# All tiles of z in pairs, scans beside 16 gate tiles at a falling pace, one feed-forward split sooner

## The chip, the cores and the metric

The kernel runs on one core of one Trainium2 chip. The metric is the device time of one execution in microseconds. TensorE does all matmuls and transposes; VectorE (DVE in the rows), ScalarE (ACT) and GpSimd (POOL) work beside it on tiles in SBUF and on PSUM banks; each of these engines works through its own instructions in the order in which the program issues them. SyncE (SP), ScalarE and GpSimd also issue DMAs. The kernel fixes the order on each engine by hand: instructions stand on an engine in the order in which the Python program calls them.

## The reference, cut to what matters

```
h  = rmsnorm(x, norm_mix_w)                       # x: 1024 rows x 1024
u  = h @ w_in                                     # z 2048, xbc 3072, dt 32, s_b, s_c, s_x, g_a, g_b 1024 each
xbc = silu(causal_conv(xbc))                      # 4 taps -> xs (2048), B, C (4 groups x 128)
y  = ssd_chunked_scan(xs, dt, a, B, C) + d_skip * xs
y  = y * silu(z)                                  # per group of 512 columns:
y  = y * rsqrt(mean(y*y) + eps) * ssd_norm_w
branch_a = y @ w_ssd_proj
branch_b = (s_b * causal_conv(s_c * s_x)) @ w_sconv_proj
h1 = x + (sigmoid(g_a) * branch_a + sigmoid(g_b) * branch_b) @ w_o
out = rmsnorm(h1 + swiglu(rmsnorm(h1)), final_norm_w)   # swiglu: silu(h@w_gate)*(h@w_up) @ w_down, 2816 wide
```

Everything is float32.

## The kernel before

**Numbers.** Every float32 product is computed as three matmuls of float32r (hi·hi, hi·lo, lo·hi: `mm3`, L80 to L83, and `mmc`, L678 to L681). Each operand is split for it by `split`: ScalarE copies the high part (L73, L76), VectorE subtracts it from the source (L74, L77). SBUF is dealt out in 47 pages of 128x1024 float32 from one pool, PSUM in 8 banks of 128x512.

**Stages**, with the time of the profiled execution.

- *Start* (0 to about 20 us): `x` is loaded by rows (the first four tiles by L231 on SP), `rows_sq` and `rows_scale` form the norm on ScalarE and VectorE, and the rows are transposed.
- *Pairs* (to 619 us): two tiles of 128 columns of `w_in` are taken together and multiplied with the normed, transposed `x` by the Strassen-Winograd scheme, in 7 products of 4 k x 3 matmuls instead of 2 tiles x 48. A `Pair` loads its two slabs, forms the sums of the blocks, splits them and evicts each product. `slots` lists all products: those of the first three z pairs interleaved, then the pairs of `rest_p` one by one, which takes in turn one of `conv_p` (xbc) and one of `free_p` (s_c, s_x, s_b, and the other z pairs, which are its end). There are 30 pairs, 6 of them for z (12 of its 16 tiles); the last three in order are z pairs.
- *Direct* (619 to 952.6 us): the last four tiles of z and the 16 tiles of g_a and g_b are computed by `direct_tile`, each in two halves of 512 rows, each half 8 k x 3 matmuls. A z tile is evicted raw by `z_raw` and every two tiles ScalarE applies silu to both; a gate tile is evicted raw and goes to DRAM. The high part of the next tile is split in the first half at k = 1, the low part at k = 7.
- *Scans* (`scans`) run beside the direct tiles. An item is one group (g of 4) and one block of 128 rows (c of 8). `part1` (L408 on) transposes xs, multiplies B with C, prepares the operands `bh`, `bl` (B^T) and `xw` (weighted xs); ahead of the next item, `prep2` (L396 to L400) computes decays on ScalarE. `part2` (L459 on) reads the former state (`poff`), forms the new one (`pst`, evicted to `st` by L482 in the first item of a group) and adds the parts of y. After every fourth item `norm` (L502 on) multiplies with silu(z), sums squares (`pq`), takes the reciprocal root (`rstd_of`, L99 to L107), transposes it (`prt`, L532), sends it to DRAM and back as a broadcast (`rbc`, two DMAs of POOL), scales y with it (L543), and at the end of a group forms four sums t1 and t2 and stores them. These generators wait in a list and advance by one step at each scan step.
- *Merge* (952.6 to 1250 us): the products with w_sconv_proj, w_ssd_proj and w_o (`gv`, `gy`, `go` in one `Stream`, Strassen-Winograd by blocks of 512), in chunks of 24 matmuls. After each chunk what is left of the scans and norms is pumped. The list `chunks` says what is split ahead. During `go`, the last, `early_weights` (L1327 to L1344) loads and splits the first weights of the feed-forward.
- *Feed-forward* (to the end): `ffn_phase`; `steps[s]` holds, for product s, the split of its weights, its matmuls and its eviction. 

**What sets the pace of the scans.** `direct_tile` counts turns (one turn is one k: three matmuls) and gives out the next scan step (`pump_scan`) whenever the count asks for it:

```
turn, SCAN_STEPS = [0, 0], 2 * G * NT + 1
due = turn[0] * SCAN_STEPS // (len(direct) * 2 * KT - 4)
if due > turn[1]:
    turn[1] = due
    pump_scan()
```

So 65 steps are spread evenly over 316 of the 320 turns. Steps 1 and 2 are the first halves of items 0 and 1, and from there second and first halves take turns (step 3 the second half of item 0, step 4 the first half of item 2).

## Time and profile before

| | |
|---|---|
| time, median of 3 runs | 1910.57 us (1910.33 to 1910.74) |
| the profiled execution's own time | 1910.68 us |
| its span in the profile | 1908.9 us |
| TensorE busy (PE) | 1879.7 us, 98% |
| weight loads of TensorE (PEld) | 81% |
| VectorE busy | 1299.4 us, 68% |
| ScalarE busy | 970.6 us, 51% |
| GpSimd busy | 9% |

The span runs from the first to the last recorded instruction. "Busy" is an average over the stages; the rows of a stage further down say more. A line number such as L679 is the line of the kernel whose instruction it is, and names such as `gb_8196` are tiles with a running number. TensorE takes up its matmuls overlapped, so that the length of one row is more than the distance to the next.

### The profile page before, as it was taken

What the parts mean: (1) busy time and instruction counts of PE and PEld (TensorE: products, weight loads), DVE (VectorE), ACT (ScalarE), POOL (GpSimd) and SP (SyncE); (2) the same over time, 40 slices, a digit from 0 to 9 for tenths busy, and PEclk for the clock granted to TensorE, in tenths of its full rate; (3) what the DMA queues carried; (4) which work ended last, traced back from release to release, by engine and by line L of the source; (5) the groups of instructions that cost most, each with busy time, mean ns of one, the idle gap of its engine ahead of it and who ended that gap; (6) DMA issues with size and microseconds to landing.
All of it is one profiled execution on the core that took longest, in us unless ns stands there. A gap on an engine that the chain in (4) does not pass through costs nothing.

```text
span 1908.9 us, 24143 instructions
## 1 busy us (share of the span) xinstructions
PE 1879.7 (98%) x8905; PEld 1545.3 (81%) x8905; DVE 1299.4 (68%) x1688; ACT 970.6 (51%) x1541; POOL 169.7 (9%) x196
## 2 busy tenths in 40 slices
PE   7999999999999999999999999999999999999998
PEld 5688888888888888888878888887888888888886
DVE  7667878777785678889878548877444444456465
ACT  5545454444444987877665454464333333345333
POOL 1010111101100000101010000101211121100000
PEclk9999999999999999999999999999999999999999
DMA  5197999978959656778798665917988888867552
GB/s 181 48 275 173 240 230 236 240 187 226 264 149 288 223 194 219 251 250 269 261 321 311 226 208 203 229 80 171 215 193 220 195 193 192 232 257 286 190 196 110
DMA packets 341190, 411.97 MB, mean 216 GB/s; under 512 B 17384, under 2 KB 223936, under 8 KB 341072
## 3 DMA queue, kind: packets, MB, share of 16 engines
q1 hardware_dynamic: 284400, 308.59, 50.0%
q0 software_dynamic: 48608, 72.47, 20.9%
q10 hardware_dynamic: 8064, 29.36, 3.8%
q8 instruction: 70, 1.15, 0.2%
q14 instruction: 48, 0.39, 0.1%
HBM read 320.56 MB, written 143.15 MB: 243 GB/s over the span
## 4 chain that ended last, share of the span: by engine, by line
PE 92%; DVE 4%; ACT 2%; DMA 1%; issue 1%; SPq 0%; ACTq 0%; DVEq 0%
PE pb L679 5%; PE pb L680 5%; PE pb L681 5%; PE gb L679 5%; PE gb L680 5%; PE gb L681 5%; PE fb L681 4%; PE fb L679 4%; PE fb L680 4%; PE pr L81 4%; PE pr L83 4%; PE pr L82 4%; PE gd L679 4%; PE pd L679 4%; PE gd L681 4%; PE gd L680 4%
## 5 line engine op out<-in xcount | busy, mean ns | idle before, releaser
L77 DVE TENSOR_TENSOR wl<-ws,wh 128x1024 fp32r<-128x1024 f32 x77 | 94.0, 1221 | 121.6 <-ACT wh L76 121.6
L679 PE MATMUL gb<-qh,gh 128*128 128x512 f32 x432 | 169.1, 391 | 1.1 <-DVE h L1132 1.1
L680 PE MATMUL gb<-ql,gh 128*128 128x512 f32 x432 | 168.9, 391 | 0.0
L681 PE MATMUL gb<-qh,gl 128*128 128x512 f32 x432 | 168.7, 391 | 0.0
L681 PE MATMUL fb<-th,wl 128*128 128x512 f32 x352 | 137.1, 389 | 0.8 <-DVE wl L77 0.8
L679 PE MATMUL fb<-th,wh 128*128 128x512 f32 x352 | 137.1, 390 | 0.6 <-ACT wh L76 0.6
L680 PE MATMUL fb<-tl,wh 128*128 128x512 f32 x352 | 137.0, 389 | 0.0
L81 PE MATMUL pr<-th,wh 128*128 128x512 f32 x320 | 131.1, 410 | 0.0
L679 PE MATMUL gd<-qh,gh 128*128 128x512 f32 x324 | 126.0, 389 | 0.0
L680 PE MATMUL gd<-ql,gh 128*128 128x512 f32 x324 | 126.0, 389 | 0.0
L681 PE MATMUL gd<-qh,gl 128*128 128x512 f32 x324 | 126.0, 389 | 0.0
L83 PE MATMUL pr<-th,wl 128*128 128x512 f32 x320 | 125.1, 391 | 0.0
L82 PE MATMUL pr<-tl,wh 128*128 128x512 f32 x320 | 124.9, 390 | 0.0
L76 ACT ACTIVATE qh<-cb 128x1024 fp32r<-128x1024 f32 x98 | 99.8, 1018 | 38.0 <-PE gb L680 17.1
L77 DVE TENSOR_TENSOR ql<-cb,qh 128x1024 fp32r<-128x1024 f32 x98 | 115.6, 1180 | 1.6 <-ACT qh L76 1.4
L74 DVE SCALAR_TENSOR_TENSOR gl<-ca,gh 128x1024 fp32r<-128x1024 f32 (+1 forms) x60 | 70.5, 1174 | 49.0 <-ACT gh L73 49.0
L681 PE MATMUL fd<-th,wl 128*128 128x512 f32 x264 | 102.7, 389 | 0.0
L679 PE MATMUL fd<-th,wh 128*128 128x512 f32 x264 | 102.7, 389 | 0.0
L680 PE MATMUL fd<-tl,wh 128*128 128x512 f32 x264 | 102.7, 389 | 0.0
L679 PEld LDWEIGHTS gb<-qh,gh 128*128 128x128 f32 x432 | 81.5, 189 | 18.4 <-DVE h L1132 1.4
L679 PE MATMUL pb<-th,wh 128*128 128x512 f32 x240 | 94.4, 394 | 1.0 <-ACT u L894 1.0
L681 PEld LDWEIGHTS gb<-qh,gl 128*128 128x128 f32 x432 | 81.5, 189 | 17.1
(324 smaller groups left out, 4702.3 us busy)
## 6 DMA issues: line engine op xcount, KB each, us to landing
ws<-in_w_in_dram SPq DMA_DIRECT2D x80, 512.0 KB, 6.3
ws<-in_w_gate_dram SPq DMA_DIRECT2D x77, 256.0 KB, 3.9
ws<-in_w_up_dram SPq DMA_DIRECT2D x77, 256.0 KB, 4.4
ca<-u_d SPq DMA_DIRECT2D x35, 512.0 KB, 5.3
ab<-ac_d SPq DMA_DIRECT2D x32, 512.0 KB, 6.0
xbc_g<-cv ACTq DMA_DIRECT2D x24, 512.0 KB, 7.0
ws<-ws POOLq DMA_DIRECT2D x22, 512.0 KB, 6.4
wd_d<-in_w_down_dram SPq DMA_DIRECT2D x20, 512.0 KB, 10.8
```

The source lines that it names most:

```text
L74: nc.vector.scalar_tensor_tensor(lo, src, -1.0, hi.bitcast(F32), op0=ALU.mult, op1=ALU.subtract)
L76: nc.scalar.activation(hi, src, AF.Copy)
L77: nc.vector.tensor_sub(lo, src, hi.bitcast(F32))
L81: nc.tensor.matmul(o, lh, rh, start=first, stop=False)
L82: nc.tensor.matmul(o, lh, rl, start=False, stop=False)
L83: nc.tensor.matmul(o, ll, rh, start=False, stop=last)
L679: nc.tensor.matmul(o, lh, rh, start=first, stop=False, skip_group_check=True)
L680: nc.tensor.matmul(o, lh, rl, start=False, stop=False, skip_group_check=True)
L681: nc.tensor.matmul(o, ll, rh, start=False, stop=last, skip_group_check=True)
```

## The change

Four edits:

1. `z_pairs` takes all 16 tiles of z. There are 32 pairs now, the last five in order are z pairs, and `direct` holds the 16 gate tiles alone. `z_raw` is gone.
2. The pace of the scan steps: over 252 of 256 turns, with a formula that gives out 15% more steps per turn at the start and 15% fewer at the end. In floating point 1.15 - 0.15 is a hair under 1, so the formula ends at 64 steps; the 65th goes to the first chunk of the merge stage.
3. `steps[3][0]`, the split of the weights of one product of the feed-forward, stands beside `steps[7][0]` in `early_weights`, before the last chunk of the merge stage, and no longer after that stage.
4. Of the four loads of `x` at the start, two are issued by ScalarE.

```diff
@@ -228,7 +228,7 @@
     for i in range(4):
-        nc.sync.dma_start(xt[i], x[i * P:(i + 1) * P, :])
+        (nc.scalar if i % 2 else nc.sync).dma_start(xt[i], x[i * P:(i + 1) * P, :])
@@ -906,7 +906,7 @@
-    z_pairs = [Pair(i * P, (silu_z(i), silu_z(i + 1))) for i in range(0, 12, 2)]
+    z_pairs = [Pair(i * P, (silu_z(i), silu_z(i + 1))) for i in range(0, 16, 2)]
@@ -957,21 +957,7 @@
-    def z_raw(i):
...
-    direct = [(wslab(w_in, i * P), z_raw(i)) for i in range(12, 16)]
+    direct = []
     for j in range(KT):
         direct += [(wslab(w_in, GA0 + j * P), gate_raw(ga_d[j])), (wslab(w_in, GB0 + j * P), gate_raw(gb_d[j]))]
@@ -1000,7 +986,8 @@
                 turn[0] += 1
-                due = turn[0] * SCAN_STEPS // (len(direct) * 2 * KT - 4)
+                at = min(turn[0] / (len(direct) * 2 * KT - 4), 1.0)
+                due = int(SCAN_STEPS * at * (1.15 - 0.15 * at))
                 if due > turn[1]:
@@ -1339,6 +1326,7 @@
             yield
             steps[7][0]()
+            steps[3][0]()
             load_to(9)
@@ -1357,7 +1345,6 @@
         steps[8][0]()
-        steps[3][0]()
         steps[1][1]()
```

**Where the first state is copied (ScalarE, early in the direct stage).** `ab` and `cd` are the decays of the next item, `st` the first state of the scan of group 0, `gt` a direct tile, `wh` the high part of the next direct tile, `bh` the operand of a later item. Before:

```order
L396 ACTIVATE cd_4741<-ab_4657 128x8
L398 ACTIVATE ab_4657<-ab_4657,pac 128x128 x8
L400 ACTIVATE ab_4657<-ab_4657 128x1024
L482 ACTIVATE st_4767<-pst_4768 128x512
L966 ACTIVATE gt_4705<-pr_4707 128x512
L987 ACTIVATE wh_4798<-ws_4636 128x1024
L436 ACTIVATE bh_4822<-pcb_4818 128x128
```

After:

```order
L396 ACTIVATE cd_4980<-ab_4906 128x8
L398 ACTIVATE ab_4906<-ab_4906,pac 128x128 x8
L400 ACTIVATE ab_4906<-ab_4906 128x1024
L656 ACTIVATE gt_4995<-pr_4875 128x512
L482 ACTIVATE st_5007<-pst_5008 128x512
L436 ACTIVATE bh_5049<-pcb_5045 128x128
```

The work of the scans ahead of the copy of the state is the same; the eviction of a direct tile that follows in the first list (its first half stands further up there) is ahead of the copy in the second, and the scan steps are fewer direct matmuls apart.

**Where the last norms meet the merge stage (VectorE).** `y` are halves of the group's result being scaled, `s` the third sum of the former group, `gv`, `gr`, `gq` the reciprocal root of the last norm, `gl` and `ql` low parts of merge chunks. Before:

```order
L543 SCALAR_TENSOR_TENSOR y_6769<-y_6769,cols,rbc_7880 128x512 x2
L557 TENSOR_TENSOR s_1240_8139<-y_6315,y_6768 128x1024
L99 TENSOR_SCALAR gv_8148<-pq_8143 128x4
L102 RECIPROCAL gr_8150<-gr_8150 128x4
L104 TENSOR_TENSOR gq_8153<-gr_8150 128x4
L105 TENSOR_TENSOR gq_8153<-gq_8153,gv_8148 128x4
L106 TENSOR_SCALAR gq_8153<-gq_8153 128x4
L107 TENSOR_TENSOR gr_8150<-gr_8150,gq_8153 128x4
L74 SCALAR_TENSOR_TENSOR gl_8181<-ca_7889,gh_8180 128x1024
L77 TENSOR_TENSOR ql_8185<-cb_7891,qh_8184 128x1024
L74 SCALAR_TENSOR_TENSOR gl_8189<-ca_8035,gh_8188 128x1024
L77 TENSOR_TENSOR ql_8193<-cb_8037,qh_8192 128x1024
```

After:

```order
L543 SCALAR_TENSOR_TENSOR y_6831<-y_6831,cols,rbc_7904 128x512 x2
L74 SCALAR_TENSOR_TENSOR gl_8169<-ca_7860,gh_8168 128x1024
L77 TENSOR_TENSOR ql_8173<-cb_7862,qh_8172 128x1024
L74 SCALAR_TENSOR_TENSOR gl_8177<-ca_8043,gh_8176 128x1024
L77 TENSOR_TENSOR ql_8181<-cb_8045,qh_8180 128x1024
L557 TENSOR_TENSOR s_1262_8213<-y_6410,y_6830 128x1024
L99 TENSOR_SCALAR gv_8222<-pq_8217 128x4
L102 RECIPROCAL gr_8224<-gr_8224 128x4
L104 TENSOR_TENSOR gq_8227<-gr_8224 128x4
L105 TENSOR_TENSOR gq_8227<-gq_8227,gv_8222 128x4
L106 TENSOR_SCALAR gq_8227<-gq_8227 128x4
L107 TENSOR_TENSOR gr_8224<-gr_8224,gq_8227 128x4
```

The sum and the root now stand behind the four splits of the second and third chunk. On TensorE the transposed root `prt` stood after the first merge chunk and stands after the second.

**At the end of the merge stage (VectorE).** `h` are the rows of h1, `wl` and `ws` weights of the feed-forward, `mc` and `cb` operands of the last merge chunk. Before:

```order
L1132 TENSOR_TENSOR h_1578_9939<-h_1578_9939,gd_10305 128x512
L77 TENSOR_TENSOR wl_10371<-ws_10325,wh_10370 128x1024
L74 SCALAR_TENSOR_TENSOR gl_10378<-mc_9442,gh_10377 128x1024
L77 TENSOR_TENSOR ql_10382<-cb_10280,qh_10381 128x1024
L1147 TENSOR_TENSOR hss_10409<-sq_166 128x4
```

After:

```order
L1119 TENSOR_TENSOR h_1584_9947<-h_1584_9947,gd_10313 128x512
L77 TENSOR_TENSOR wl_10379<-ws_10333,wh_10378 128x1024
L77 TENSOR_TENSOR wl_10383<-ws_10144,wh_10382 128x1024
L74 SCALAR_TENSOR_TENSOR gl_10390<-mc_9450,gh_10389 128x1024
L77 TENSOR_TENSOR ql_10394<-cb_10288,qh_10393 128x1024
L1134 TENSOR_TENSOR hss_10421<-sq_166 128x4
```

One more split of weights stands ahead of the splits of the last chunk and of the sum of squares of h1; ScalarE gets the high part of the same weights in the same place.

## Rows read from the trace of the kernel before

**Rows 1.** The page of the profiled execution: busy time, share of the span and instructions of the engines, and by engine the chain of work that ended last.

```profile
PE 1879.7 (98%) x8905; PEld 1545.3 (81%) x8905; DVE 1299.4 (68%) x1688; ACT 970.6 (51%) x1541; POOL 169.7 (9%) x196
...
PE 92%; DVE 4%; ACT 2%; DMA 1%; issue 1%; SPq 0%; ACTq 0%; DVEq 0%
```

**Rows 2.** Busy time by stretch of the span (from:to in us, length, then busy time of each engine with its instructions, the granted clock, the DMA share and GB/s): the pair stage, the merge stage from its eighth microsecond on, the start of the feed-forward.

```profile
76.00:560.00 484.00, 482.76 (x2122) 396.99 (x2122) 361.77 (x425) 224.16 (x300) 53.24 (x62) 1.00 0.87 219
...
960.00:1250.00 290.00, 287.88 (x1268) 237.79 (x1267) 209.67 (x223) 148.42 (x174) 16.34 (x20) 0.99 0.75 247
1250.00:1320.00 70.00, 67.51 (x329) 56.07 (x328) 55.91 (x68) 42.37 (x64) 6.92 (x6) 1.00 0.37 92
```

**Rows 3.** What TensorE waited for: engine, line and tile <- what it waited for, then us, times, longest.

```profile
PE prt L532 <- DVE gr L107: 2.1, 1, 2.1
```

**Rows 4.** Timeline of TensorE at the start of the merge stage: start and length in us, line, tile written <- tiles read, shape, count [idle time before, and what ended it].

```profile
977.77 0.39 PE L680 MATMUL gb<-ql,gh 128*128 128x512 f32 x1
...
980.72 0.39 PE L681 MATMUL gb<-qh,gl 128*128 128x512 f32 x1
983.22 0.27 PE L532 MATMUL prt<-ident,gr 128*4 128x128 f32 x1 [2.12 <-DVE gr L107]
...
984.31 0.63 PE L680 MATMUL gb<-ql,gh 128*128 128x512 f32 x1
984.74 0.63 PE L681 MATMUL gb<-qh,gl 128*128 128x512 f32 x1
...
987.30 0.55 PE L681 MATMUL gb<-qh,gl 128*128 128x512 f32 x1
```

**Rows 5.** Timeline of TensorE at the start of the direct stage (first matmul at 618.97): the first instruction of the first five scan steps.

```profile
622.37 0.38 PE L426 MATMUL pxt<-ident,bc 128*128 128x128 f32 x2
...
626.61 0.38 PE L426 MATMUL pxt<-ident,bc 128*128 128x128 f32 x2
...
630.79 0.39 PE L81 MATMUL pst<-xw,bh 128*128 128x512 f32 x1
...
636.12 0.38 PE L426 MATMUL pxt<-ident,bc 128*128 128x128 f32 x2
...
640.36 1.05 PE L475 MATMUL poff<-bc,st 128*128 128x128 f32 x8
```

**Rows 6.** Timeline of ScalarE in the same place: the first work of the scans, and the copy of the first state.

```profile
622.23 2.43 ACT L398 ACTIVATE ab<-ab,pac 128x128 f32<-128x128 f32 x8
...
638.49 0.58 ACT L482 ACTIVATE st<-pst 128x512 f32<-128x512 f32 x1
```

**Rows 7.** Timeline of VectorE in the same place: the low part of xw of the first item.

```profile
628.77 0.68 DVE L450 TENSOR_TENSOR xw<-xx,xw 128x512 fp32r<-128x512 f32 x1
```

**Rows 8.** Busy time by stretch again: the direct stage, and 125 us of it in which norms run beside the scans.

```profile
619.00:952.70 333.70, 333.70 (x2064) 275.55 (x2063) 277.90 (x472) 263.82 (x611) 19.72 (x30) 1.00 0.73 238
...
772.00:897.00 125.00, 125.00 (x779) 103.52 (x778) 111.55 (x188) 97.30 (x230) 11.97 (x18) 1.00 0.78 257
```

**Rows 9.** Timeline of TensorE where the merge stage begins: its first matmul, and the transposed root of norm (3,0).

```profile
952.56 0.39 PE L679 MATMUL gb<-qh,gh 128*128 128x512 f32 x1
...
958.00 0.27 PE L532 MATMUL prt<-ident,gr 128*4 128x128 f32 x1
```

**Rows 10.** Timeline of POOL: the two small DMAs of a norm (the root to DRAM, and its broadcast back), in the direct stage and at the start of the merge stage.

```profile
759.72 0.53 POOL L536 DMA_DIRECT2D rs_d<-rst  x1 [15.57 <-ACT rst L534]
763.78 0.58 POOL L538 DMA_DIRECT2D rbc<-rs_d  x1 [3.53 <-DMA rs_d<-rst]
...
965.03 0.53 POOL L536 DMA_DIRECT2D rs_d<-rst  x1
972.20 0.57 POOL L538 DMA_DIRECT2D rbc<-rs_d  x1 [6.64 <-PE gd L681]
```

**Rows 11.** Timeline of VectorE at the start of the merge stage: the first split there, the scaling by the broadcast root, and the split of chunk 6.

```profile
954.85 1.23 DVE L74 SCALAR_TENSOR_TENSOR gl<-ca,gh 128x1024 fp32r<-128x1024 f32 x1 [3.45 <-ACT gh L73]
...
979.12 2.74 DVE L543 SCALAR_TENSOR_TENSOR y<-y,cols,rbc 128x512 f32<-128x512 f32 x4 [2.89 <-DMA rbc<-rs_d]
...
986.49 1.22 DVE L77 TENSOR_TENSOR ql<-cb,qh 128x1024 fp32r<-128x1024 f32 x1
```

**Rows 12.** Timeline of ScalarE, VectorE and TensorE at the end of the merge stage (wh, wl: weights of the feed-forward; gh, gl: a merge chunk), and one row of VectorE later in the feed-forward.

```profile
1242.22 1.04 ACT L76 ACTIVATE wh<-ws 128x1024 fp32r<-128x1024 f32 x1
...
1243.30 1.23 DVE L77 TENSOR_TENSOR wl<-ws,wh 128x1024 fp32r<-128x1024 f32 x1 [1.74 <-ACT wh L76]
1244.44 1.22 DVE L74 SCALAR_TENSOR_TENSOR gl<-mc,gh 128x1024 fp32r<-128x1024 f32 x1
...
1254.60 0.50 PE L679 MATMUL gb<-qh,gh 128*128 128x512 f32 x1 [1.13 <-DVE h L1132]
...
1305.31 2.36 DVE L77 TENSOR_TENSOR tl<-br,th 128x1024 fp32r<-128x1024 f32 x2 [1.94 <-ACT th L76]
```

**Rows 13.** The loads of x: from issue to landing for the four of L231; then VectorE's square of the last of the four rows, and the copy of the constants and the root on ScalarE.

```profile
DMA to landing us min/median/max: 3.3/5.5/7.7
...
9.86 1.23 DVE L115 SCALAR_TENSOR_TENSOR xn<-x 128x1024 f32<-128x1024 f32 x1 [3.13 <-DMA x<-in_x_dram]
...
10.70 0.32 ACT L1534 ACTIVATE cols<-pc 128x176 f32<-128x176 f32 x1 [1.14 <-PE pc L1533]
11.41 0.20 ACT L101 ACTIVATE nr<-nv 128x4 f32<-128x4 f32 x1 [0.39 <-DVE nv L99]
```

More of the change, by code (lines that the diff above doesn't have):

```diff
@@ L957, in slot @@
         p.ev(n)
-    z_held = []
-    def z_raw(i):
-        def f(ps, hf):
-            if hf == 0:
-                z_held.append((i, page("gt")))
-            nc.scalar.activation(z_held[-1][1][:, hf * 512:hf * 512 + 512], ps, AF.Copy)
-            if hf and len(z_held) == 2:
-                for k, t in z_held:
-                    nc.scalar.activation(t, t, AF.Silu)
-                    nc.scalar.dma_start(z_d[k], t)
-                z_held.clear()
-        return f
-    direct = [(wslab(w_in, i * P), z_raw(i)) for i in range(12, 16)]
+    direct = []
     for j in range(KT):
```

## The prediction

> **What bounds the kernel now.** The page first: TensorE is busy for 1879.7 of 1908.9 us and the chain of waits that ended last runs through it for 92% of the span [rows 1]. The windows by stage then show where the other 29 us are: the pair stage (76 to 560) stands still for 1.24 us of 484, the merge stage (960 to 1250) for 2.1 us of 290, the start of the feed-forward (1250 to 1320) for 2.5 us of 70 [rows 2]; the rest is the load at the start and the tail. So this kernel gains by fewer matmuls, and loses by every wait that TensorE doesn't have today. The list of what TensorE waited for names, among the single stops that the change can reach, 2.1 us on a reciprocal root of a norm [rows 3]; the other is 1.13 us on an addition at the end of the merge stage [rows 12]. The price of a matmul is its pace, not its duration, since matmuls overlap: 13 of them from 977.77 to 980.72 are 0.227 us each [rows 4].
>
> **Four tiles of z move into pairs.** A direct tile is 2 halves x 8 k x 3 = 48 matmuls, four are 192. A pair is 7 products x 4 k x 3 = 84, two are 168. The 24 that go are 24 x 0.227 = **5.45 us less**. Each new pair brings VectorE about 9.9 us (an estimate: three passes of 128x1024 at 1.23 [rows 12] and nine of 128x512 at 0.68 [rows 7]) beside 84 x 0.227 = 19.1 us of TensorE, in a stage where VectorE is busy for 361.77 us of 484 [rows 2]: nothing. Four direct splits, four silus and their switches of ScalarE's table leave the direct stage.
>
> **Scans beside 16 tiles: the first items.** I call the three matmuls of one k a turn (0.681 us). A scan step was given out at turns 5, 10, 15, 20 and 25; by the new formula at 4, 7, 11, 14 and 18. Steps 1, 2 and 4 are the first halves of items 0, 1 and 2, steps 3 and 5 the second halves of items 0 and 1. TensorE met them at 622.37, 626.61, 630.79, 636.12 and 640.36 [rows 5]; a first half took 626.61 - 622.37 - 5 x 0.681 = 0.835 us, step 3 took 5.33 - 3.405 = 1.925. ScalarE meanwhile worked with hardly a gap from 622.23 until it copied the first state at 638.49 to 639.07 [rows 6]. The instructions ahead of that copy stay the same in number, so the copy stays at 639.1 by the clock of today's stage (which begins at 618.97); only TensorE comes sooner. Step 3: 618.97 + 11 x 0.681 + 2 x 0.835 = 628.1; its second matmul needs the low part of xw, which VectorE finished at 628.77 + 0.68 = 629.45 [rows 7]. That is a stop of 629.5 - 628.4 = 1.16 us where 1.3 us were to spare. Step 5: 628.1 + 1.16 + 1.925 + 3 x 0.681 + 0.835 + 4 x 0.681 = 636.8; it reads the state, ready at 639.1: a stop of 2.3 us. Together **3.46 us more**; 2.5 if VectorE and ScalarE, entered sooner by TensorE, save a wait, 4.0 if the copy slips. After that ScalarE catches up: it is busy for 263.82 of today's 333.70 us [rows 8], and of the eighth of the time that goes it loses its own share with the z tiles.
>
> **The middle of the scans.** VectorE is busy for 277.90 of the 333.70 us of the direct stage [rows 8]; without four splits of 1.22 [rows 11] that is 273, and TensorE's part falls by 192 x 0.227 to 290: 94%. In the densest stretch VectorE has 111.55 us in 125 [rows 8], that is 24.6 steps of 5.08 us; less 7.5 splits, 4.16 us per step, and 4.43 with the splits at the new pace. TensorE needs (333.7 - 217.9) / 65 = 1.78 us per step and 2.64 / slope beside it: 4.14 at slope 1.12, 4.43 at 1.0, 4.88 at 0.85. Between step 10 (before it there is no norm) and step 35 VectorE thus falls behind by 0.15 x 25 = 3.7 us and then recovers. TensorE asks for a state two steps (8.6 us) after the step that makes it, and that lies 2 us inside VectorE's work, so a lag of 6 us does no harm. I take 0; the other end is the whole 3.7.
>
> **The norms at the start of the merge stage.** The formula ends at 65 x (1.15 - 0.15), which in floating point is just under 65, so 64 steps are given out where 65 were: everything after is one step later in the merge chunks (24 matmuls, 5.45 us each). Today, counted from the first merge matmul at 952.56: the transposed root of norm (3,0) leaves TensorE at 958.00 [rows 9], its DMA is issued at 965.03, the broadcast at 972.20 [rows 10] and has landed at 979.12, where VectorE stands 2.89 us for it; the next norm's root and the split of chunk 6 queue behind, the split ends at 986.49 + 1.22 [rows 11], 8.6 us after the landing. TensorE waits 2.12 us for the root at 983.22; from 984.31 to 987.30 its matmuls start 0.43 apart, half the pace [rows 4], eight of them, 1.6 us: 3.7 us in all. In the changed order the transpose stands after the second chunk, not the first, and ahead of its DMA POOL holds the third sum's, whose addition VectorE reaches after four splits (from +2.3 to +6.85), a sum, the root's chain (+9.4), a sum, two products (+12.8) and two splits (+15.1): +16.2. DMA at +16.95, then the same 7.2 and 6.9 us: landed at +31.0, split of chunk 6 ready at +39.6. TensorE asks for it at 6 x 5.45 + two sums of squares (1.6) + two transposes (0.5) + 0.23 = +35.0. So the stop at the root goes, and one of up to 4.6 us at chunk 6 takes its place, with the 1.6 us behind it: **+2.5 us** against today. If both DMAs land sooner than in those two rows by 4.6 us in all, nothing stops: **-3.7 us**. The first is the nearer row, the other the longer reach; I take 0.
>
> **One split of the feed-forward sooner.** It adds one pass on ScalarE behind the one at 1242.22 and one on VectorE behind the one at 1243.30 [rows 12]. Behind them queue, in the chain of waits itself: the split of a merge chunk, the norm's root, the scaled rows, the next chunk's split and the addition that frees TensorE's bank. A pass of VectorE there takes 1244.44 - 1243.30 = 1.14 us, and TensorE already stands 1.13 us at 1254.60 for the end of it [rows 12]: **1.14 us more**, a stop of 2.27. Today's 2.12 us were followed by half pace, the 1.13 us were not; by the nearer row I add **1.6 us**, the other end is 0. What is taken away at 1276 gives nothing: TensorE doesn't wait there, and its next wait, after 1310, hangs on a chain for which VectorE itself stood idle 1.94 us at 1305.31 [rows 12].
>
> **Rows of x on two queues.** The four loads were issued 0.43 us apart and landed 3.3 to 7.7 us later [rows 13]. The last reaches VectorE at 9.86, and the root on ScalarE is at 11.41; but ScalarE must first copy the constants at 10.70 for 0.32 us [rows 13], so at most 0.39 us are won. ScalarE can issue only after its table load and one pass, at 2.2 us instead of 1.2: up to 1.05 us lost. I take 0. The Trainium skill (DMA: Bandwidth & Descriptors, "Issuing engines are not separate DMA queues") says that loads of all issuing engines run on the same 16 DMA engines and interleave, so only issue time is saved; by that rule this edit is worth 0 here, by the rows between -0.4 and +1.05, and no run shows yet which.
>
> **Sum.** -5.45 + 3.46 + 0 + 0 + 1.14 + 1.6 + 0 = +0.75 us. The profiled execution took 1910.68 us (span 1908.9 and 1.8 around it), 0.1 above the median; on the median of 1910.57 this gives **1911.3 us**, no change that a measurement of this kernel can tell (0.2% is 3.8 us).
>
> **Rivals.** First, *both stops stay away*: the two small DMAs of the norm land sooner at the lighter end of the direct stage, and the 2.27 us don't pull the clock down: -5.45 + 3.46 - 3.7 + 1.14 = -4.55, 1906.0 us. For it: the same pair of DMAs took 4.1 us where the first was issued at 759.72 and the second at 763.78 [rows 10]. Against: DMA engines are busier in the merge stage. Second, *VectorE becomes the bound* in the middle of the direct stage, slower: if its lag of 3.7 us isn't taken up by the two steps between halves (a bank or a page that is handed on late decides it, from a lag of about 4 us on), TensorE stands for it: 1911.3 + 3.7 = 1915.0 us. For it: 94% of an engine that waits in order; against: today's stretch of 89% costs TensorE nothing, all of its 125 us are busy [rows 8]. Third, *the change doesn't do what it says*: TensorE doesn't wait at the first items, because something else in ScalarE's queue leaves sooner: 1911.3 - 3.46 = 1907.8, still no change that can be told, or with the first rival 1902.5.
>
> **Chances.** My forecast with the third rival alone 0.60, the first (alone or with the third) 0.24, the second 0.16. The range reaches to the first rival with its bounds (1905.0: 1906.0 and the 2.5 for 3.46) and to the second with the upper ends of the other terms (1916.0), leaving out the sum of all losses. Faster by over 0.2% is only the lower part of it, below 1906.75: 0.24; within 0.60; slower 0.16.
>
> **What would show it.** 24 matmuls fewer, at the same pace. In the first 20 us of the direct stage TensorE stops at pst for 1.2 and at poff for 2.3 us; none there refutes that term. At the start of the merge stage no stop at the transpose of the root, and one at the low part of chunk 6, 0 to 4.6 us long. At the end of the merge stage 2.3 us before the same matmul as today. Any stop in the middle of the direct stage that names VectorE speaks for the second rival. Wrong altogether I would be if the pair stage, which stood still for 1.24 us only, had to wait for z stores or weights.

## The result, and the profile after

The changed kernel is slower: 1915.96 us median of 9 runs (1912.21 to 1917.24) against 1910.57 of the kernel before, measured again beside it (9 runs, 1908.44 to 1910.75). The ratio is 1.0033, 95% interval 1.0024 to 1.0041. The forecast was 1911.3 us and no change that can be told; the median lies at the very end of its range, and the way it moved was given 16%.

The profiled execution took 1917.24 us, the slowest of the nine; its span is 1915.2 us, 6.3 more than that of before. The page, first the busy times, then the chain of waits by engine, answers to [rows 1]:

```profile
PE 1880.7 (98%) x8881; PEld 1542.8 (81%) x8881; DVE 1311.2 (68%) x1708; ACT 966.1 (50%) x1543; POOL 169.4 (9%) x196
...
PE 85%; DVE 6%; ACT 5%; DMA 2%; issue 2%; SPq 0%; ACTq 0%; POOL 0%; DVEq 0%; POOLq 0%
```

24 matmuls fewer, yet TensorE is busy for 1.0 us more, and the chain runs through it for 85% of the span instead of 92%. The windows by stage (columns as in [rows 2]) say where: the gate tiles with the scans, the merge stage.

```profile
655.90:952.20 296.30, 292.81 (x1864) 239.18 (x1863) 267.94 (x461) 242.99 (x589) 18.94 (x29) 0.99 0.76 251
960.00:1250.00 290.00, 285.46 (x1255) 235.31 (x1254) 208.63 (x221) 147.57 (x175) 17.06 (x21) 0.99 0.76 248
```

The direct stage, which stood still nowhere before [rows 8], loses 3.5 us, the merge stage 4.5 where it lost 2.1. What TensorE waited for (columns as in [rows 3]) has five rows in the reach of the change, six stops (the one at poff counts two), where there were two:

```profile
PE gd L680 <- DVE ql L77: 3.2, 1, 3.2
...
PE poff L475 <- ACT st L482: 2.3, 2, 1.8
PE gb L679 <- DVE h L1119: 2.3, 1, 2.3
PE pq L527 <- DVE mc L1039: 1.4, 1, 1.4
...
PE pst L82 <- DVE xw L450: 1.0, 1, 1.0
```

**The start of the direct stage.** Timeline of TensorE (answers to [rows 5]; the stage begins at 655.90):

```profile
666.44 0.50 PE L82 MATMUL pst<-xw,bh 128*128 128x512 f32 x1 [1.05 <-DVE xw L450]
...
676.05 1.70 PE L475 MATMUL poff<-bc,st 128*128 128x128 f32 x8 [1.76 <-ACT st L482]
677.40 0.77 PE L81 MATMUL pst<-xw,bh 128*128 128x512 f32 x1
677.97 0.63 PE L82 MATMUL pst<-xw,bh 128*128 128x512 f32 x1
678.40 0.63 PE L83 MATMUL pst<-xw,bl 128*128 128x512 f32 x1
```

The low part of xw ends 10.48 us after the stage began (VectorE, L450: 665.70 + 0.68), which is what it was before; the state is copied by 676.00 (ScalarE, L482: 675.41 + 0.59), 20.1 us after, again as before. TensorE alone came sooner and stands for both. Behind the second stop its matmuls run at half pace until 680.4: in the window from 676 to 681 the granted clock is 0.66, so the lower of its two levels, 1.2 GHz, for much of it. From the start of this poff to the next matmul of a direct tile it takes 4.38 us (to 680.43) where it took 2.70 before: 1.7 us more.

**The start of the merge stage** (first matmul at 952.18). Timeline of TensorE, answers to [rows 4, 9]:

```profile
964.01 0.27 PE L532 MATMUL prt<-ident,gr 128*4 128x128 f32 x1
...
976.57 1.05 PE L527 MATMUL pq<-ones,sa 128*128 128x1 f32 x8 [1.39 <-DVE mc L1039]
...
992.42 0.50 PE L680 MATMUL gd<-ql,gh 128*128 128x512 f32 x1 [3.15 <-DVE ql L77]
...
994.30 0.63 PE L681 MATMUL gd<-qh,gl 128*128 128x512 f32 x1
994.73 0.63 PE L679 MATMUL gd<-qh,gh 128*128 128x512 f32 x1
```

and of POOL and VectorE, answers to [rows 10, 11]:

```profile
969.39 0.53 POOL L536 DMA_DIRECT2D rs_d<-rst  x1
976.90 0.56 POOL L538 DMA_DIRECT2D rbc<-rs_d  x1 [6.98 <-issue]
```

```profile
983.77 2.74 DVE L543 SCALAR_TENSOR_TENSOR y<-y,cols,rbc 128x512 f32<-128x512 f32 x4 [5.47 <-DMA rbc<-rs_d]
...
991.15 1.22 DVE L77 TENSOR_TENSOR ql<-cb,qh 128x1024 fp32r<-128x1024 f32 x1
```

The root's DMA is issued 17.2 us after the first merge matmul, the broadcast lands after 31.6, VectorE having stood 5.47 us for it, and the split that queues behind is ready after 40.2. TensorE stands 3.15 us for that split, runs six matmuls at its usual pace and then eight about 0.43 us apart; in the window from 993.90 to 997.30 the granted clock is 0.51.

**The end of the merge stage**, answers to [rows 12]:

```profile
1259.25 0.50 PE L679 MATMUL gb<-qh,gh 128*128 128x512 f32 x1 [2.26 <-DVE h L1119]
...
1260.82 0.63 PE L681 MATMUL gb<-qh,gl 128*128 128x512 f32 x1
1261.25 0.63 PE L679 MATMUL gb<-qh,gh 128*128 128x512 f32 x1
```

**The load of x**, answers to [rows 13]: the queue of ScalarE (ACTq) issues its two DMAs while ScalarE loads its table, and the last row reaches VectorE at 8.56.

```profile
0.75 1.28 ACT L229 ACT_TABLE_LOAD   x1 [0.75 <-PEq L1703]
0.95 0.87 ACTq L231 DMA_DIRECT2D x<-in_x_dram  x2
...
8.56 1.23 DVE L115 SCALAR_TENSOR_TENSOR xn<-x 128x1024 f32<-128x1024 f32 x1 [1.71 <-DMA x<-in_x_dram]
```

**The account.** The same instructions of TensorE in both traces, read at five places, give the shift of the profiled execution:

```
place (TensorE)                     before     after    shift   of it here, against what the forecast had
first direct matmul                 618.97    655.90   +36.93   168 x 0.227 = 38.14 expected: start -1.2 (0)
first merge matmul                  952.56    952.18    -0.38   stage -43.58 by fewer matmuls, +6.27 lost (3.46)
merge matmul 160                    993.83    997.29    +3.46   +3.84 (0)
first feed-forward matmul          1267.38   1273.66    +6.28   +2.82 (2.74)
last matmul                        1901.22   1907.46    +6.24   0 (0)
```

-5.45 - 1.21 + 6.27 + 3.84 + 2.82 = +6.27 us (that the loss of the direct stage and the whole sum are the same number is chance). The median moved by 5.4 us; the profiled execution was the slowest of the nine.

### The profile page after: what moved, and what is told of

It is laid out like the page before. It is cut to its first block, busy times and chain, and to the rows that moved or that the text cites. A ratio compares the mean times of both kernels' runs of the same rounds, so it can differ in the third digit from the quotient of the medians.

```text
span 1915.2 us, 24103 instructions
## 1 busy us (share of the span) xinstructions
PE 1880.7 (98%) x8881; PEld 1542.8 (81%) x8881; DVE 1311.2 (68%) x1708; ACT 966.1 (50%) x1543; POOL 169.4 (9%) x196
## 3 DMA queue, kind: packets, MB, share of 16 engines
q8 instruction: 70, 1.15, 0.2%
## 4 chain that ended last, share of the span: by engine, by line
PE 85%; DVE 6%; ACT 5%; DMA 2%; issue 2%; SPq 0%; ACTq 0%; POOL 0%; DVEq 0%; POOLq 0%
PE pb L679 6%; PE pb L680 6%; PE pb L681 6%; PE gb L679 5%; PE gb L680 5%; PE gb L681 5%; PE pd L679 4%; PE pd L680 4%; PE pd L681 4%; PE fb L681 4%; PE fb L679 4%; PE fb L680 4%; PE gd L680 4%; PE gd L681 4%; PE gd L679 4%; PE fd L679 3%
## 5 line engine op out<-in xcount | busy, mean ns | idle before, releaser
L81 PE MATMUL pr<-th,wh 128*128 128x512 f32 x256 | 106.3, 415 | 0.0
L864 ACT ACTIVATE wh<-ws 128x1024 fp32r<-128x1024 f32 x64 | 67.8, 1059 | 67.3 <-DVE ws L851 63.1
L679 PE MATMUL pb<-th,wh 128*128 128x512 f32 x256 | 100.6, 393 | 0.5 <-ACT u L894 0.5
L680 PE MATMUL pb<-tl,wk 128*128 128x512 f32 x256 | 99.7, 390 | 0.8 <-DVE tl L77 0.8
L679 PE MATMUL pb<-th,wk 128*128 128x512 f32 x256 | 99.8, 390 | 0.7 <-ACT th L76 0.4
L680 PE MATMUL pb<-tl,wh 128*128 128x512 f32 x256 | 99.9, 390 | 0.5 <-DVE tl L77 0.5
```

What stands on the lines that cost most here:

```text
L81: nc.tensor.matmul(o, lh, rh, start=first, stop=False)
L679: nc.tensor.matmul(o, lh, rh, start=first, stop=False, skip_group_check=True)
L680: nc.tensor.matmul(o, lh, rl, start=False, stop=False, skip_group_check=True)
L864: nc.scalar.activation(t[0], self.source(what), AF.Copy)
```

## The experiments

Each kernel differs from the changed one by the diff shown. Ratios are to the kernel before, timed on the same chip with it.

**1. 65 steps instead of 64.**

```diff
-                due = int(SCAN_STEPS * at * (1.15 - 0.15 * at))
+                due = int(SCAN_STEPS * at * (1.15 - 0.15 * at) + 1e-9)
```

> The pace formula is rounded so that it gives out 65 steps beside the gate tiles, not 64. Theory (the stops of TensorE at the start of the merge stage come from the norms standing one step later): the norm's root is transposed after the first merge chunk again, its broadcast lands some 4 to 5 us sooner, and the merge stage loses what it lost before (2.1 us at the root and 1.6 us of half pace) instead of the 7.5 us of the changed kernel: 3.84 us less, 1912.1 us from 1915.96. Rival (the time is lost in the direct stage, where VectorE is the bound, and the merge stage only shows it): the 65th step lengthens the direct stage by what it takes from the merge stage, and the time stays at 1915.5 to 1916.5.

Measured: 1.0013 (1.0004 to 1.0022), median 1911.50 of 11 runs. The theory holds: 0.0020 less is 3.8 us (the two intervals leave 1.5 to 6). Timeline of TensorE at the start and at the end of the merge stage of this kernel:

```profile
981.95 0.27 PE L532 MATMUL prt<-ident,gr 128*4 128x128 f32 x1 [2.01 <-DVE gr L107]
...
983.69 0.40 PE L680 MATMUL gb<-ql,gh 128*128 128x512 f32 x1
983.92 0.39 PE L681 MATMUL gb<-qh,gl 128*128 128x512 f32 x1
...
1252.86 0.50 PE L679 MATMUL gb<-qh,gh 128*128 128x512 f32 x1 [2.27 <-DVE h L1119]
```

The stop at the split of chunk 6 is gone, the one at the root is back, as before. The direct stage takes 295.79 us instead of 296.28, with one step more in it. Those two can't be set side by side as they are, since half pace follows the stop at poff in the changed kernel and not here; experiment 3, with 64 steps and no half pace there either, takes 294.65. So the 65th step lengthens the direct stage by 1.1 us, most of it a sum of squares of 0.78, and not by the 3.8 us that the rival asks for: the rival falls. What is new: none of the stops of this execution is followed by half pace (behind the root's the matmuls start 0.23 apart; the granted clock from 982 to 985.5 is 1.00), and the runs of this one kernel spread from 1908.95 to 1913.98.

**2. An even pace, 65 steps.**

```diff
-                due = int(SCAN_STEPS * at * (1.15 - 0.15 * at))
+                due = int(SCAN_STEPS * at + 1e-9)
```

> All 65 steps at an even pace over the 252 turns: steps 1 to 5 at turns 4, 8, 12, 16 and 20 where the changed kernel has 4, 7, 11, 14 and 18. Theory (stops where TensorE comes before the low part of xw and before the copy of the first state, and half pace behind the longer one): TensorE comes 0.68 us later to each, so the stops shrink from 1.05 and 1.76 us to 0.4 and 1.1, and the half pace behind the second (1.8 us) goes: 3.1 us less, and with the 65th step's 3.84 it gives 1909.0 us. Rival (a pace that falls is needed, because the norms at the end wait for the last items): the start gains its 3.1 us and the last norms in the direct stage and at the start of the merge stage give it back: 1912 us or more.

Measured: 1.0062 (1.0050 to 1.0075), median 1920.85. The theory was right on the start and wrong on the kernel, whose time is the rival's (1912 us or more). The first two stops shrink to 0.38 and 0.38 us, with a new one of 0.72 between them that names VectorE, but the direct stage now takes 304.60 us. TensorE late in it:

```profile
892.80 1.16 PE L475 MATMUL poff<-bc,st 128*128 128x128 f32 x8 [2.32 <-ACT st L482]
...
949.50 2.05 PE L475 MATMUL poff<-bc,st 128*128 128x128 f32 x8 [3.83 <-DVE st L484]
...
992.58 0.27 PE L532 MATMUL prt<-ident,gr 128*4 128x128 f32 x1 [3.81 <-DVE gr L107]
```

and the window from 870 to 900 of this kernel, in which VectorE has 29.42 us of work in 30:

```profile
870.00:900.00 30.00, 27.09 (x165) 21.79 (x165) 29.42 (x51) 25.76 (x65) 4.69 (x7) 0.94 0.78 269
```

So the falling pace is no ornament: beside 16 tiles it is worth 8.8 us of the direct stage against the even one (304.60 - 295.79, one profiled execution each).

**3. The feed-forward split back behind the merge stage.**

```diff
             steps[7][0]()
-            steps[3][0]()
...
         steps[8][0]()
+        steps[3][0]()
         steps[1][1]()
```

> The changed kernel with the split of the third product's weights put back behind the merge stage. Theory (the split lengthens the chain through VectorE that TensorE waits for at the end of the merge stage): the stop there shrinks from 2.26 us to 1.13 and the 1.6 us of half pace behind it go, nothing comes back later: 1913.2 us. Rival (moving it bought something in the feed-forward that hides this): a new stop of 1 to 2.7 us between 1260 and 1330 and no change, 1915.5 to 1916.5.

Measured: 1.0017 (1.0009 to 1.0026), median 1911.62; 0.0016 less is 3.1 us, the 2.7 that the theory gave, within the intervals. The stop at the end of the merge stage is 1.13 us again, without half pace behind it, and the feed-forward has the two stops it had, 0.58 and 0.78 us. Edit 3 costs its time and buys nothing.

**4. The rows of x by SP alone.**

```diff
-        (nc.scalar if i % 2 else nc.sync).dma_start(xt[i], x[i * P:(i + 1) * P, :])
+        nc.sync.dma_start(xt[i], x[i * P:(i + 1) * P, :])
```

> The changed kernel with all four rows of x loaded by SP again. Theory (the two rows issued by ScalarE, at 0.95 us while it loads a table, let the last row reach VectorE at 8.56 instead of 9.86): the first transposes start 1.2 us later again: 1917.2 us. Rival (issuing engines share the DMA engines, and what differed at the start is the spread between executions): no difference, 1915.5 to 1916.5.

Measured: 1.0039 (1.0026 to 1.0051), median 1916.60. The times alone can't decide: the interval holds both answers. The traces can. The first direct matmul starts at 656.82 here and at 656.86 in experiment 12, the two kernels with all rows on SP; with the rows on two queues it starts between 655.54 and 656.05 in all eleven other profiles with 32 pairs. The edit is worth about 1 us.

**5. The first states copied by VectorE** (with 65 steps).

```diff
             if c == 0:
-                nc.scalar.activation(ns, pst, AF.Copy)
+                V.tensor_copy(ns, pst)
```

> The changed kernel with 65 steps, and the first state of each group copied by VectorE instead of ScalarE. Theory (TensorE stops at poff because that copy stands behind the decays of the next item on ScalarE): the stop of 1.75 us at the fifth step, the half pace behind it where there is any (0.7 to 1.8 us) and the stop of 0.5 us at the last group's first state go; 2.5 to 4 us less than the kernel with 65 steps alone, 0.9990 to 1.0000 of the kernel before. Rival (VectorE, busy for 29.3 of 30 us in the dense part, is what TensorE ends up waiting for): the four copies of 0.7 us come back as stops that name VectorE, the time stays at 1.0005 to 1.0020.

Measured: 0.9996 (0.9987 to 1.0005), median 1909.26. The theory holds: the direct stage falls from 295.79 to 292.65 us, the stops at poff behind ScalarE's copy are gone (a first and a last row of what is left; the stop at pst stays), and what VectorE gives back is small:

```profile
666.59 0.50 PE L82 MATMUL pst<-xw,bh 128*128 128x512 f32 x1 [1.06 <-DVE xw L450]
940.05 1.16 PE L475 MATMUL poff<-bc,st 128*128 128x128 f32 x8 [0.45 <-DVE st L484]
```

**6. All of it together**: 65 steps, the copy on VectorE, the split back, and the low part of xw ahead of the product with the decays; z in pairs, the falling pace and the two queues stay.

```diff
         ab = bufs.pop(j)
-        V.tensor_mul(ab, ab, cbm.unsqueeze(1).to_broadcast([P, HPG, P]))
         if not last:
             V.tensor_sub(xw[:, 1], xwf, xw[:, 0].bitcast(F32))
             ops = bh, bl, xw
+        V.tensor_mul(ab, ab, cbm.unsqueeze(1).to_broadcast([P, HPG, P]))
```

> 65 steps, the first states copied by VectorE, the low part of xw ahead of the decays' product on VectorE, and the feed-forward split back where it was; z in pairs and the two queues for x stay. Theory (each stop is a loss of its own, and nothing else is): no stop at pst and poff at the start of the direct stage, at the merge stage's start and end the losses of the kernel before; 24 matmuls (5.45 us) and the start (1.2 us) are left as gain: 6.0 us less than the kernel before, 0.9965 to 0.9975. Rival (VectorE is the bound of the direct stage at 16 tiles): the direct stage still takes over 293 us from its first to its last matmul, and the ratio is 0.9985 or more.

Measured: 0.9985 (0.9976 to 0.9994), median 1907.17 of 11 runs: the lowest ratio here, 2.9 us faster than the kernel before, but half of what the theory gave. Waits of TensorE in its trace that came or stayed:

```profile
PE prt L532 <- DVE gr L107: 3.0, 1, 3.0
...
PE pr L83 <- DVE wl L976: 0.7, 1, 0.7
```

The swap won nothing that the trace shows: the stop of 1.06 us at pst became 0.40 at pdg, which reads the product that now comes later, and 0.69 at a direct tile's split. Most of the gain that is missing lies in the direct stage: it takes 292.98 us, where that of the kernel before less 192 matmuls would take 333.59 - 43.58 = 290.0. So the rival, with its 293 us and 0.9985, came as near as the theory.

At the root TensorE waits 3.04 us where it waited 2.12. It reaches the merge stage 3.66 us sooner than before, but that is not the reason: in experiment 5 it comes there sooner still, at 948.70 against 948.90, and the stop is 1.77. In both, GpSimd issues the root's DMA 12.5 us after the first merge matmul. What differs is how long that DMA takes; here are the two DMAs of the norm, first in experiment 5, then in this one:

```profile
961.18 0.53 POOL L536 DMA_DIRECT2D rs_d<-rst  x1
968.35 0.56 POOL L538 DMA_DIRECT2D rbc<-rs_d  x1 [6.63 <-PE gd L681]
...
961.37 0.53 POOL L536 DMA_DIRECT2D rs_d<-rst  x1
970.00 0.57 POOL L538 DMA_DIRECT2D rbc<-rs_d  x1 [8.10 <-PE gd L681]
```

The broadcast reads what the root's DMA wrote, so the step from one to the other, 7.17 and 8.63 us, is that DMA (the matmul that the profile names had long been done).

**7. The even pace with less work for VectorE.** The additions of the scans' results to y are left out except in the first item of each group, so y lacks them.

```diff
-            V.tensor_add(y[i], y[i], src)
+            if c == 0:
+                V.tensor_add(y[i], y[i], src)
...
-                due = int(SCAN_STEPS * at * (1.15 - 0.15 * at))
+                due = int(SCAN_STEPS * at + 1e-9)
```

> The even pace once more, with the additions of the scans' results to y left out except in the first item of each group (28 times two additions on VectorE, 21 us of its work; y then lacks them). Theory (at the even pace VectorE falls behind and TensorE waits for it late in the direct stage): the stops of 2.3 us at 893 and 3.8 us at 949.5 and the half pace behind them go, the direct stage shrinks from 304.4 to 291 to 293 us. Rival (it is ScalarE's order, where the copy of a state stands behind the decays and a weight's split): the stops stay and the stage takes over 300 us.

Measured: one run, 1913.35 us; the direct stage takes 296.62 us. The stops between 883 and 893 are gone, among them the one that names ScalarE's copy, so that one too came from VectorE's lag, though ScalarE is named; the one at the end became 2.40 us at 942.66, again for VectorE's addition to the state. 8 of the 12 or so us that the theory gave came: the 296.62 lie between the theory's 293 and the rival's 300. VectorE is the main cause of experiment 2, and whether the rest is its alone stays open.

**8. A slow start, then the falling pace** (65 steps).

```diff
-                due = int(SCAN_STEPS * at * (1.15 - 0.15 * at))
+                b = (turn[0] - 25) / (len(direct) * 2 * KT - 29)
+                due = turn[0] // 5 if b <= 0 else 5 + int((SCAN_STEPS - 5) * min(b, 1.0) * (1.15 - 0.15 * min(b, 1.0)) + 1e-9)
```

> The first five steps at turns 5, 10, 15, 20 and 25 as in the kernel before, and the other 60 at a pace that falls from 1.15 to 0.85 over the remaining 227 turns. Theory (the first stops come from the pace of the first five steps alone): no stop at pst and poff at the start, 2.8 us and up to 1.8 us of half pace less than the kernel with 65 steps, which is 0.9990 to 1.0000 of the kernel before. Rival (the steps that are late at the start must be made up while VectorE is full, so its lag moves to the end): stops of 2 us and more that name VectorE or a state after 880, and 1.0010 or more.

Measured: 1.0029 (1.0017 to 1.0040), median 1915.10. The theory falls, the rival holds, in another place than it said. No stop is left at pst or poff at the start, but the direct stage takes 298.43 us, and:

```profile
816.77 2.07 PE L475 MATMUL poff<-bc,st 128*128 128x128 f32 x8 [4.08 <-ACT st L482]
...
986.78 0.37 PE L532 MATMUL prt<-ident,gr 128*4 128x128 f32 x1 [3.95 <-DVE gr L107]
```

The first stops are the price of the steps that must be early; of the two kernels, the one that pays it at the start (experiment 1, 1.0013) is the cheaper.

**9. The stores of the groups' four sums by SP** (with all of experiment 6).

```diff
-            nc.gpsimd.dma_start(yt_d[f][256 * g:256 * g + 256, :].rearrange("(k p) f -> p k f", p=P), t)
+            nc.sync.dma_start(yt_d[f][256 * g:256 * g + 256, :].rearrange("(k p) f -> p k f", p=P), t)
```

> The best kernel so far (65 steps, states copied by VectorE, low part of xw first, feed-forward split back) with the stores of the groups' four sums issued by SP, so that on GpSimd the norm's root no longer stands behind them. Theory (the merge stage starts with a stop because the root's first DMA waits on GpSimd for a sum of VectorE: issued at 961.4 us where the root had left TensorE some 7 us earlier): the broadcast lands 5 to 7 us sooner, the stop of 3.0 us at the next root and the half pace behind it go, 3.0 to 4.6 us less, 0.9960 to 0.9972 of the kernel before. Rival (SP waits for the sums in front of its loads, and the operands of the merge stage come late): stops on DMAs at the start of the merge stage, 0.9985 or more.

Measured: 0.9995 (0.9986 to 1.0003), median 1909.39; the times can't tell it from experiment 6 (0.9976 to 0.9994), the traces can. Both happened. GpSimd issues the root's DMA at 959.37 and the broadcast at 963.89, 6.3 and 10.8 us after the first merge matmul, where it was 12.5 and 21.1 in experiment 6; the stop at the root falls to 0.71 us, one of 1.12 comes at the sum of squares, and from the first merge matmul to the first of the feed-forward it takes 313.09 us instead of 315.56. But SP waits for a sum of an earlier group in front of a load: the store goes out at 817.16 and the load of x behind it at 820.07 (814.52 in experiment 6). The direct stage takes 297.03 us instead of 292.98:

```profile
828.96 0.44 PE L426 MATMUL pxt<-ident,x 128*128 128x128 f32 x2 [2.90 <-DMA x<-xbc_g]
...
983.57 0.27 PE L532 MATMUL prt<-ident,gr 128*4 128x128 f32 x1 [0.71 <-DVE gr L107]
```

**10. A steeper pace** (with all of experiment 6).

```diff
-                due = int(SCAN_STEPS * at * (1.15 - 0.15 * at) + 1e-9)
+                due = int(SCAN_STEPS * at * (1.25 - 0.25 * at) + 1e-9)
```

> The same best kernel with a steeper pace, from 1.25 to 0.75 of the even one. Theory (TensorE waits at the end of the direct stage, 0.6 us at 940, because VectorE carries a lag there; a slower end takes it up, and the start has room now that ScalarE's copy is off its path): the stop at 940 goes, the one at the root (3.0 us) shrinks by up to as much as VectorE gets ahead, 0.9972 to 0.9985 of the kernel before. Rival (the first items can't go faster, since ScalarE works on the decays without a gap there): new stops before 690 us that cost 2 us or more, 0.9990 or more.

Measured: 1.0014 (1.0005 to 1.0024), median 1913.28. Neither as put, but the ratio is the rival's (0.9990 or more) and the stops before 690 us add up to 1.9 of its 2 us. The stop at 940 goes; but there are stops at the start (0.23, 0.23, 0.41 and 1.06 us before 675) and seven more between 772 and 905, of 0.19 to 1.11 us, all naming VectorE. The direct stage takes 298.83 us, 5.9 more than in experiment 6. Between a pace that is even (experiment 2) and one that falls from 1.25 to 0.75, the changed kernel's slope is the better place.

**11. Only the third group's sums stored by SP** (with all of experiment 6).

```diff
-            nc.gpsimd.dma_start(yt_d[f][256 * g:256 * g + 256, :].rearrange("(k p) f -> p k f", p=P), t)
+            (nc.sync if g == 2 else nc.gpsimd).dma_start(yt_d[f][256 * g:256 * g + 256, :].rearrange("(k p) f -> p k f", p=P), t)
```

> The best kernel so far, with only the third group's four sums stored by SP (those that stand at the start of the merge stage), the others by GpSimd. Theory (the stop at the last norm's root hangs on the root's first DMA standing behind these stores on GpSimd; the stop of 2.9 us at 829 in the run before came from an earlier group's sums in front of a load on SP): no stop at 829, the stop of 3.0 us at the root falls to about 0.7, a stop of 1.1 at the sum of squares comes new: 1 to 3 us less, 0.9970 to 0.9980 of the kernel before. Rival (at the start of the merge stage the loads behind the stores on SP decide): stops of 3 us and more there, 0.9985 or more.

Measured: 0.9989 (0.9980 to 0.9998), median 1907.36: not to be told from experiment 6. The stop at 829 is gone and so is the one at the root, all of it. In its place stands one at the sum of squares, with eleven matmuls 0.43 us apart behind it:

```profile
972.73 1.71 PE L527 MATMUL pq<-ones,sa 128*128 128x1 f32 x8 [1.74 <-DVE mc L1039]
```

The rival's mechanism is the one behind it, at 1.7 us instead of 3: on SP a load for a merge chunk stands behind the store of 960.44 and goes out at 960.89 (957.88 in experiment 6), ScalarE waits 2.79 us for it, and VectorE comes to the eviction that the sum of squares waits for at 972.00 instead of 970.09. From the first merge matmul to the first of the feed-forward it is 315.97 us, 315.56 in experiment 6.

**12. Edits 1 and 2 alone**, as the change has them (64 steps): the split and the loads of x as in the kernel before (the diffs of experiments 3 and 4 together).

> The changed kernel with the feed-forward split and the loads of x as they were: the four tiles of z in pairs and the falling pace with its 64 steps alone. Theory (the edits add up): the changed kernel's 1.0033 of the kernel before, less the split's 2.7 us, plus 1.2 for the loads of x: 1.0020 to 1.0030. Rival (without the other edits the 24 matmuls saved are left over): 0.9975 to 1.0005.

Measured: 1.0021 (1.0012 to 1.0030), median 1913.61. The edits add up, and the 24 matmuls are not left over: 5.45 us saved, and more lost.

## Why the prediction was wrong, step by step

**What bounds the kernel, and 24 matmuls: right.** They are gone at 0.227 us each; the pair stage paid nothing for two more pairs (the windows from 76 to 560 stand still 0.74 us, before 1.24).

**Scans beside 16 tiles, the first items: mechanism right, one term left out.** The stops were forecast as 1.16 and 2.3 us, at pst and at poff, and measured as 1.05 and 1.76: the arithmetic by ScalarE's clock, with TensorE alone coming sooner, holds to some half a microsecond. But the 1.6 us of half pace that I added behind the stop at the end of the merge stage I did not add behind this one, though it is as long as the row I took that from. It came, 1.7 us: 4.5 instead of 3.46. It need not come: in experiments 1 and 3 the same stop of 1.75 or 1.76 us has no half pace behind it. Experiment 5 shows the cause of the larger stop: without ScalarE's copy it is gone.

**The middle of the scans: 0 taken, 1.8 measured** (2.6, less the 0.78 of a sum of squares that moved to the merge stage). The second rival, TensorE standing 3.7 us for VectorE there, did not happen; experiments 2, 8 and 10 show how near it was. About half of the 2.6 is the copy of the state once more, which each of the four groups has and I counted once. In the second and third group TensorE starts poff when ScalarE has ended the copy (743.85 + 0.58, 814.93 + 0.58):

```profile
743.85 0.58 ACT L482 ACTIVATE st<-pst 128x512 f32<-128x512 f32 x1
814.93 0.58 ACT L482 ACTIVATE st<-pst 128x512 f32<-128x512 f32 x1
...
744.48 1.16 PE L475 MATMUL poff<-bc,st 128*128 128x128 f32 x8
815.56 1.16 PE L475 MATMUL poff<-bc,st 128*128 128x128 f32 x8
```

The list of waits names only the stop of the last group, 0.59 us at 889.79. By distance between the starts of matmuls the four cost 1.9, 0.2, 0.1 and 0.7 us, 3.0 together, of which 1.76 stands in the first term. About 1.2 us remain that no wait accounts for; many small distances between matmuls are a little longer, and why stays open.

**The norms at the start of the merge stage: this is the step that failed.** The chain was worked out right: broadcast landed at +31.0 (measured +31.6), split of chunk 6 ready at +39.6 (+40.2), a stop of up to 4.6 us there (1.39 at the sum of squares and 3.15 at the split, with half pace behind). It gave +2.5 us by the DMA times of the rows next to it [rows 10], and -3.7 by a pair of DMAs from the middle of the direct stage. I then took 0, which is neither: a value between two cases that exclude each other, and I had called the first the nearer row. It was +3.84: the stops together, 4.54 us, are what was forecast, and of the 1.3 us beyond +2.5 the sum of squares that moved here from the direct stage is 0.78. Experiment 1 shows the cause: with the 65th step given out in the direct stage all of it goes. By the times, a rounding of 1.15 - 0.15 costs 3.8 us here.

Why the near row was the right one: the two DMAs took 7.5 and 6.9 us (7.2 and 6.9 forecast), and what counts is what stands in front. Just ahead of the root's DMA GpSimd has issued a store of a sum, and the root lands when that store does. In experiment 6 that store lands 8.6 us after 960.65 and the root 8.1 us after 961.37, in experiment 5 7.2 after 960.46 and 6.6 after 961.18; in experiments 9 and 11, where SP has these stores, the step from the root's DMA to the broadcast is 4.5 and 4.8 us, although the DMA engines are as busy (their share is 0.98 and 1.04 meanwhile, 0.97 in the changed kernel). The row of 4.1 us from the direct stage has no store just ahead of it either.

**One split sooner: right**, 1.14 + 1.6 forecast, 2.82 in the trace, 3.1 by the times of experiment 3.

**Rows of x: 0 taken, -1.2 measured.** The step that failed is "ScalarE can issue only after its table load and one pass": the row of ACTq shows the two DMAs issued at 0.95, during the load. The bound of 0.39 us on the gain failed too: the copy of the constants, which stood at 10.70, comes at 9.97. The Trainium skill (DMA: Bandwidth & Descriptors, "Issuing engines are not separate DMA queues") has it that only issue time is saved. The trace agrees with the way, but the 0 that I drew from it doesn't follow: SP alone took 1.82 us for the four issues, each queue took 0.87 for two, and the last row reached VectorE 1.3 us sooner.

**The sum.** With +2.5 in place of 0 and the half pace behind poff, the same working gives 0.75 + 2.5 + 1.6 = +4.85 us, 1915.4; the median came out at 1915.96. That it is so near is in part luck: 1.8 us in the middle of the scans and 1.3 more at the norms are not in it, 1.2 us at the start went the other way, the two first stops were 0.65 shorter, and the median is 1.3 us below the profiled execution whose terms these are. Neither the first rival (both stops stay away) nor the third (no wait at the first items) came. The chances went wrong with the sum: what cost most was in view and had been set to 0.

## What to carry to other kernels

Where a bound has a near row and a far one and the two exclude each other, take one and leave the other to a rival; a value between them is a case that can't occur. When work beside TensorE is squeezed into fewer matmuls, look first for instructions that keep their own clock (here a copy behind a queue on ScalarE, done 20.1 us after the stage began before and after): what TensorE gains ahead of them is waited for there. A chain that starts from TensorE's own work, as the norm's round trip through DRAM, moves with TensorE; there the order decides, and what its DMAs queue behind. And an integer count that is worked out in floating point is to be read at its last value.

## What the runs showed of the hardware

The same stop is followed by half pace in one execution and not in another. The stop of 2.26 or 2.27 us at the end of the merge stage costs another 1.6 us in the changed kernel and in experiments 2, 4, 5, 7 and 8, and nothing in experiment 1; the stop at the root has it before (2.12 us) and not in experiment 1 (2.01) nor in experiment 5 (1.77). Windows of TensorE's stretches behind stops, in the changed kernel:

```profile
993.90:997.30 3.40, 3.40 (x10) 2.60 (x9) 3.40 (x4) 2.57 (x3) 0.00 (x0) 0.51 0.97 369
1260.80:1263.80 3.00, 3.00 (x9) 2.39 (x8) 1.51 (x3) 2.16 (x6) 0.00 (x0) 0.54 0.00 0
```

and behind the root's stop in experiment 1:

```profile
982.00:985.50 3.50, 3.50 (x16) 2.88 (x17) 3.50 (x4) 3.50 (x6) 0.53 (x1) 1.00 1.01 250
```

Stops of 1.13 us and less were never followed by it in these profiles at the end of the merge stage; one of 1.38 at the sum of squares was in experiment 3 and wasn't in experiments 4 and 12, nor that of 1.39 in the changed kernel. What decides is not settled here. The runs without a trace point the same way: the kernel before was timed 85 times beside the experiments, and the 49 executions with a mean granted clock of 0.999 took 1908.8 us (median), the 36 with 0.998 took 1910.6, 1.9 us more, about what one stretch of half pace costs. That it is the stretch behind the root's stop that comes and goes there is argued, not shown: one execution of that kernel has a trace. That the runs of one kernel lie up to 5.0 us apart fits it too.

A small DMA that GpSimd issues behind a 512 KB store never lands ahead of it in these profiles. At the start of the merge stage the norm's root, issued 0.7 us behind such a store, takes 6.6 to 9.0 us and lands 0.2 to 0.4 us after it in the twelve kernels that have the store there; in experiments 9 and 11, which haven't, it takes 4.0 and 4.3 us. Elsewhere, with no store of GpSimd under way, it took 1.6 to 6.5 us.

ScalarE's queue issues DMAs while ScalarE itself loads a table (0.95 us, beside a load from 0.75 to 2.03).
